# Normalising the first stage's input before the projections, fewer decay transfers, and bias tables on 128 partitions in a hybrid decoder step

## The chip, the cores and the metric

The kernel runs on one core of a Trainium2 chip. The metric is the device time of one execution in microseconds (us). PE is TensorE's matmul side, PEld its weight load, DVE is VectorE, ACT ScalarE, POOL GpSimd, and SP the engine whose queue issues most DMAs. Traces come from one execution under the hardware profiler.

## The reference

One inference step for a prompt of 512 positions and 8 samples of 4 new positions (544 columns together), width 1024, two layers. Layer A is a Mamba-2 SSD mixer, layer B an attention mixer over three dilated windows with one K/V computed after layer A. Cut to what matters here:

```python
def rmsnorm(x, g):
    y = x * lax.rsqrt(jnp.mean(x * x, axis=-1, keepdims=True) + NORM_EPS)
    return y * g

def ssd_mixer(h, conv_prev, ssm_init, g_norm, w_in, conv_w, conv_b, dt_bias, a_log, ...):
    u = rmsnorm(h, g_norm) @ w_in            # z, x|B|C and dt
    ...                                      # conv of width 4 over x|B|C, then silu
    dt = softplus(dt_raw + dt_bias)
    y, s_final = ssd_scan(xs * dt, dt * -exp(a_log), bm, cm, ssm_init)

def ssd_scan(xdt, adt, bm, cm, init):        # chunks of 128 positions
    a_cs = jnp.cumsum(A, axis=-1)
    seg = jnp.exp(jnp.where(tri, a_cs[..., :, None] - a_cs[..., None, :], -jnp.inf))
    chunk_decay = jnp.exp(a_cs[..., -1])
    ...

def group_bias(rel_bias, g):                 # a bias for each distance and head
    return rel_bias[:, g * KV_HEADS:(g + 1) * KV_HEADS][t5_bucket(dist)]
```

## The kernel before

Activations lie transposed, 1024 channels as 8 tiles of 128 partitions by 544 columns, and are worked on in two parts, columns 0 to 255 (HA) and 256 to 543. Each f32 product is made of three passes over split operands: a high part (xh, whi) rounded to the fast matmul type and the remainder (xl, wlo): high by high, high by low, low by high. A weight tile (`fetch_w`, L185; 512 KB into one of three `wraw` buffers) is split by ACT (whi, L196) and DVE or POOL (wlo, L197). One weight tile over all columns is 48 matmul steps.

**The first stage** (L299 to L457) makes the first three conv tiles, `first = [16, 20, 0]`. Its order is written out and held. It multiplies x by the gain only (`raw_high`, `raw_low`), and runs the passes on that; the squares are summed meanwhile, the inverse norm is spread over partitions with a matmul against a diagonal (`rstd_fin`, rp), and the products are multiplied by it when they leave PSUM (`evac`, cb). Then x is normalised in place (`x_mul`, L377) and split again (`x_high` L381, `x_low` L385) for `dt_proj` and all later tiles. POOL takes a part of the low splits (POOL_A, POOL_B) and the first weights' wlo. After `dt_proj` come four z passes and then conv and z tiles (`filler_a`).

**The decays** (`dt_chain`, L474 to L510) are computed on 128 partitions, 32 heads by four chunks. What every partition must see goes through DRAM: acd and ecd (prompt rows of t2 and t3), asd and esd (sample columns, 4 DMAs each), eld (last elements, 4 + 1 DMAs, one element at a time), and back as m, ea, as, es (per unit) and dec (once, broadcast). SP issues in order, and takes one of eight completion counters in turn for each DMA, so that an issue waits until the DMA eight places before it has landed. The SSD units (`ssm_chunk`, `ssm_quad`) start with transposes xp; `ms` (L728) is the first use of `as` on DVE.

**The bias tables** (`bias_tables`, L878 to L927) run in steps between the output and K/V projections: the table relt (96 columns, 32 a group, of which 8 are heads) times one-hot columns gives biases on 32 partitions. DVE copies them into ov (prompt, two halves) and bsr (samples), which share one buffer `tv`; rows 0 to 7 are written to bvd (each head 32 times) and bsd, and read back per head in layer B. xk (L858) is x for the residual.

An unwritten order is set by the framework's scheduler from the dependencies and its own estimates. The score loop of the samples (`sample`, L1193) runs over the key ranges outside and the four samples inside.

Of the kernel before, what the change touches and what calls it, by code (L numbers as in the profile page):

```python
# [12 lines left out]
F32 = mybir.dt.float32  # L13
# [5 lines left out]
D = 1024  # L19
SEQ = 512  # L20
# [102 lines left out]
def tile_yoco_step(  # L123
# [16 lines left out]
    def mm(*a, **k):  # L140
        pin(nc.tensor.matmul(*a, **k))  # L141
# [135 lines left out]
    acd = dram.tile([128, 128], F32, name="acd")  # L277
    ecd = dram.tile([128, 128], F32, name="ecd")
    asd = dram.tile([NH, 32], F32, name="asd")
    esd = dram.tile([NH, 32], F32, name="esd")  # L280
    eld = dram.tile([12, NH], F32, name="eld")
# [17 lines left out]
    dma(x_t[1][:, :, 0:HA], xT[:, 4:8, 0:HA])  # L299
    w_raw.append(fetch_w(w_in[1]))  # L300
    for i in range(2):
        dma(x_t[i][:, :, HA:T], xT[:, 4 * i:4 * i + 4, HA:T])
    w_raw.append(fetch_w(w_in[2]))
# [17 lines left out]
    def x_square(i, c0, c1):  # L321
        hold(nc.scalar.activation(sqx[i][:, :, c0:c1], x_t[i][:, :, c0:c1], AF.Square))

    def x_sum(i, c0, c1):
        sq = sqx[i][:, :, c0:c1]
        hold(nc.vector.tensor_tensor(sq[:, 0:2], sq[:, 0:2], sq[:, 2:4], op=ALU.add))
        hold(nc.vector.tensor_tensor(sq[:, 0], sq[:, 0], sq[:, 1], op=ALU.add))

    def x_means(ms, i, c0, c1, one=False):
        n = c1 - c0  # L330
        b0s = [min(128 * b, n - 128) for b in range((n + 127) // 128)]
        for b, b0 in enumerate(b0s):
            mm(ms[:, b:b + 1], sqx[i][:, 0, c0 + b0:c0 + b0 + 128], inv_d, start=i + b == 0, stop=one or i == 1,
               skip_group_check=True)
        return ms, n, b0s

    def evac(o, p, rs):
        if rs is None:
            nc.scalar.copy(o, p)  # L339
        else:  # L340
            hold(nc.vector.tensor_tensor(o, p, rs, op=ALU.mult))

# [3 lines left out]
    def conv_in(ti, pa, rs=None):  # L346
# [4 lines left out]
        evac(cb[:, 3:3 + HA], pa[:, 0:HA], None if rs is None else rs[:, 0:HA])  # L351
        return cb, cs

    def conv_in2(cbs, pb, rs=None):
        cb, cs = cbs
        evac(cb[:, 3 + HA:3 + SEQ], pb[:, 0:SEQ - HA], None if rs is None else rs[:, HA:SEQ])
        evac(cs[:, :, 3:7], by_row(pb, SEQ - HA), None if rs is None else by_row(rs, SEQ))
# [7 lines left out]
    def raw_high(k0, k1, c0, c1):  # L365
        for k in range(k0, k1):
            hold(nc.scalar.activation(part(x_h, k, c0, c1), part(x_t, k, c0, c1), AF.Copy, scale=g_a[:, k:k + 1]))

    def raw_low(k0, k1, c0, c1):
        for k in range(k0, k1):  # L370
            hold(nc.vector.scalar_tensor_tensor(part(x_l, k, c0, c1), part(x_t, k, c0, c1), g_a[:, k:k + 1],  # L371
                                                f32(part(x_h, k, c0, c1)), op0=ALU.mult, op1=ALU.subtract))

    def x_mul(k0, k1, c0, c1):
        for k in range(k0, k1):
            xk = part(x_t, k, c0, c1)
            hold(nc.vector.scalar_tensor_tensor(xk, xk, g_a[:, k:k + 1], rs_x[:, c0:c1], op0=ALU.mult, op1=ALU.mult))  # L377

    def x_high(c0, c1):
        for k in range(KD):  # L380
            hold(nc.scalar.activation(part(x_h, k, c0, c1), part(x_t, k, c0, c1), AF.Copy))  # L381

    def x_low(c0, c1, pool):
        for k in range(KD):
            hold((nc.gpsimd if k in pool else nc.vector).tensor_tensor(  # L385
                part(x_l, k, c0, c1), part(x_t, k, c0, c1), f32(part(x_h, k, c0, c1)), op=ALU.subtract))

    def passes(p, w, c0, c1, one=True, two=True, low_last=False):
        hi, lo = w
        o = p[:, 0:c1 - c0]  # L390
        second, third = ((lo, x_h), (hi, x_l)) if low_last else ((hi, x_l), (lo, x_h))
        for k in range(KD if one else 0):
            mm(o, hi[:, k, :], part(x_h, k, c0, c1), start=k == 0, stop=False)
            mm(o, second[0][:, k, :], part(second[1], k, c0, c1), start=False, stop=False)
        for k in range(KD if two else 0):
            mm(o, third[0][:, k, :], part(third[1], k, c0, c1), start=False, stop=k == KD - 1)

    def sums_of(c0, c1):
        ms = pss("ms")
        for i in range(2):  # L400
            sums = x_means(ms, i, c0, c1)
        return sums

    dga, dgb = tt("dgx"), tt("dgx")
    rs_x = const.tile([128, T], F32, name="rstd", tag="rstd", bufs=2)
    pinned[0] = True
    raw_high(0, 4, 0, HA)
    w_first = [split_w(w_raw[0], None, nc.gpsimd, True)]
    raw_high(4, 8, 0, HA)
    raw_low(0, 8, 0, HA)  # L410
    for i in range(2):
        x_square(i, 0, HA)
        x_sum(i, 0, HA)
    w_first.append(split_w(w_raw[1], None, nc.gpsimd, True))
    pp = [pj("pa"), pj("pb"), pj("pa")]
    passes(pp[0], w_first[0], 0, HA)
    x_square(0, HA, T)
    rpa = rstd_fin(*sums_of(0, HA), dga, later=True, keep=hold)
    raw_high(0, 4, HA, T)
    raw_low(0, 4, HA, T)  # L420
    w_first.append(split_w(w_raw[2], half("w2", F32R, (128, 2, 8, 128)), nc.gpsimd, True))
    passes(pp[1], w_first[1], 0, HA)
    hold(nc.scalar.copy(rs_x[:, 0:HA], rpa()[:, 0:HA]))
    x_square(1, HA, T)
    raw_high(4, 8, HA, T)
    passes(pp[2], w_first[2], 0, HA)
    cbs = [conv_in(first[i], pp[i], rs_x) for i in range(2)]
    x_sum(0, HA, T)
    raw_low(4, 8, HA, T)
    x_sum(1, HA, T)  # L430
    x_mul(0, 2, 0, HA)
    hold(nc.gpsimd.tensor_scalar(cvp, cvp, 0.5, None, op0=ALU.mult))
    hold(nc.gpsimd.tensor_scalar(g_gate, g_gate, 0.5, None, op0=ALU.mult))
    w_more = [split_w(fetch_w(w_in[3]), None, nc.gpsimd, True)]
    pb0 = pss("pb0")
    passes(pb0, w_first[0], HA, T, True, False)
    rpb = rstd_fin(*sums_of(HA, T), dgb, later=True, keep=hold)
    hold(nc.scalar.activation(warm, epst, AF.Tanh))
    passes(pb0, w_first[0], HA, T, False, True)
    hold(nc.scalar.copy(rs_x[:, HA:T], rpb()[:, 0:HB]))  # L440
    x_mul(2, 8, 0, HA)
    conv_in2(cbs[0], pb0, rs_x)
    cbs.append(conv_in(first[2], pp[2], rs_x))
    x_high(0, HA)
    x_mul(0, 8, HA, T)
    pb1 = pj("pb")
    passes(pb1, w_first[1], HA, T)
    conv_in2(cbs[1], pb1, rs_x)
    x_low(0, HA, POOL_A)
    w_more.append(split_w(fetch_w(w_in[4]), None, nc.gpsimd, True))  # L450
    pb2 = pj("pb")
    passes(pb2, w_first[2], HA, T)
    x_high(HA, T)
    x_low(HA, T, POOL_B)


    t0, t1, t2, t3, t4 = (tm[:, 136 * i:136 * i + 136] for i in range(1, 6))  # L457
    pads = tm[:, 816:1200].rearrange("p (a b) -> p a b", b=128)
    tok = ac.tile([128, 6, 3, NH], F32, name="tok")
# [14 lines left out]
    def dt_chain():  # L474
# [23 lines left out]
        dma(acd, t2[:, 0:128])  # L498
        dma(ecd, t3[:, 0:128])
        for j in range(4):  # L500
            rows = slice(32 * j, 32 * j + 32)
            dma(asd[:, 8 * j:8 * j + 8], t2[rows, 128:136])
            dma(esd[:, 8 * j:8 * j + 8], t3[rows, 128:136])
            dma(dap(eld, (4 + 2 * j) * NH, [[1, NH], [NH, 2]]), t3[rows, 131:136:4])
        dma(dap(eld, 0, [[1, 128], [1, 1]]), t3[:, 127:128])
        dma(dec, dap(eld, 0, [[0, 128], [1, 12 * NH]]))
# [4 lines left out]

    def tok_transposes():
        tp = pss("tp", (128, 4, 128))
# [99 lines left out]
    def ssm_chunk(g, c):  # L613
# [7 lines left out]
        dma(m_t, dap(acd, (32 * c + 8 * g) * 128, [[0, 128], [128, 8], [1, 128]]))  # L621
# [21 lines left out]
        if c:  # L643
            ea = wk.tile([128, 4, 128], F32, name="ea", bufs=1)
            for s in range(2):
                dma(ea[64 * s:64 * s + 64], dap(ecd, (32 * c + 8 * g + s) * 128, [[0, 64], [256, 4], [1, 128]]))
# [27 lines left out]
    def ssm_quad(g, q):  # L674
        xs, v, G = xs_t[g], v_t[g], grp[g]
        hs = slice(8 * g, 8 * g + 8)
        if q == 0:
# [118 lines left out]
    conv_in2(cbs[2], pb2, rs_x)  # L796
# [703 lines left out]
```

## Time and profile before

| | |
|---|---|
| median of 3 runs | 1017.63 us (1017.35 to 1018.21) |
| the profiled execution | 1013.88 us |
| its span, first to last instruction | 1012.0 us |
| mean granted TensorE clock | 0.972 |
| PE busy | 944.4 us, 93% of the span |
| DVE, ACT, POOL busy | 590.5, 446.1, 249.7 us |
| DMA moved | 159.93 MB, mean 158 GB/s |

Busy time is a sum over stages with different limits, so the table says only that PE is the engine to follow. What to read is where PE is idle, what ended each idle time, and at which clock it worked after it. An inferred releaser is the last event that a wait was waiting for. Rows of the timeline give start, duration, engine, line, operation, output and input, size and count, and in brackets the idle time before.

### The profile page before, as it was taken

What the parts mean: (1) busy time and instruction counts of PE and PEld (TensorE: products, weight loads), DVE (VectorE), ACT (ScalarE), POOL (GpSimd) and SP (SyncE); (2) the same over time, 40 slices, a digit from 0 to 9 for tenths busy, and PEclk for the clock granted to TensorE, in tenths of its full rate; (3) what the DMA queues carried; (4) which work ended last, traced back from release to release, by engine and by line L of the source; (5) the groups of instructions that cost most, each with busy time, mean ns of one, the idle gap of its engine ahead of it and who ended that gap; (6) DMA issues with size and microseconds to landing.
All of it is one profiled execution on the core that took longest, in us unless ns stands there. A gap on an engine that the chain in (4) does not pass through costs nothing.

```text
span 1012.0 us, 21657 instructions
## 1 busy us (share of the span) xinstructions
PE 944.4 (93%) x8811; PEld 872.6 (86%) x8811; DVE 590.5 (58%) x1216; ACT 446.1 (44%) x940; POOL 249.7 (25%) x344
## 2 busy tenths in 40 slices
PE   5895999899999998999756999999999999999996
PEld 5894888799888888999756999998888888888896
DVE  5983897998998797554432445334433434455532
ACT  6464745556555654322211223434344434445442
POOL 4641434834744633011000420000000000000451
PEclk9898999999999999999887999999999999999998
DMA  8126254354465532446454653666566567564412
GB/s 276 49 33 150 85 194 150 136 182 143 150 200 170 178 122 96 134 158 105 155 123 126 186 180 122 248 219 204 198 211 196 190 213 225 175 209 147 157 37 89
DMA packets 68171, 159.93 MB, mean 158 GB/s; under 512 B 19304, under 2 KB 33016, under 8 KB 67560
## 3 DMA queue, kind: packets, MB, share of 16 engines
q1 hardware_dynamic: 63096, 144.27, 45.7%
q10 hardware_dynamic: 2880, 9.44, 2.3%
q0 software_dynamic: 2096, 4.84, 1.8%
q8 instruction: 69, 1.13, 0.5%
q14 instruction: 30, 0.25, 0.1%
HBM read 134.83 MB, written 21.59 MB: 155 GB/s over the span
## 4 chain that ended last, share of the span: by engine, by line
PE 77%; DVE 9%; DMA 8%; ACT 2%; issue 2%; SPq 2%; POOL 0%; DVEq 0%; ACTq 0%
PE pa L141 28%; PE pb L141 27%; PE sp L141 3%; DMA bvd<-ov 3%; PE so L141 3%; PE pv L141 2%; PE s L141 2%; DMA xk<-xT 2%; DVE co L540 1%; PE yd L141 1%; DVE x L377 1%; PE csp L141 1%; DVE wlo L197 1%; PE w L144 1%; DMA as<-asd 1%
## 5 line engine op out<-in xcount | busy, mean ns | idle before, releaser
L197 DVE TENSOR_TENSOR wlo<-wraw,whi 128x1024 fp32r<-128x1024 f32 x99 | 123.8, 1251 | 89.7 <-ACT whi L196 89.4
L196 ACT ACTIVATE whi<-wraw 128x1024 fp32r<-128x1024 f32 x105 | 110.8, 1055 | 143.1 <-PE pb L141 90.4
L141 PE MATMUL pa<-xh,whi 128*128 128x256 f32 (+1 forms) x320 | 94.0, 296 | 10.3 <-ACT whi L196 8.3
L141 PE MATMUL pb<-xh,whi 128*128 128x288 f32 (+1 forms) x304 | 91.6, 303 | 3.9 <-ACT cb L339 3.9
L141 PE MATMUL pb<-xl,whi 128*128 128x288 f32 (+1 forms) x304 | 91.5, 303 | 0.0
L141 PE MATMUL pa<-xh,wlo 128*128 128x256 f32 (+1 forms) x320 | 90.7, 290 | 0.7 <-DVE wlo L197 0.7
L141 PE MATMUL pa<-xl,whi 128*128 128x256 f32 (+1 forms) x320 | 88.6, 291 | 0.5 <-DVE xl L371 0.5
L141 PE MATMUL pb<-xh,wlo 128*128 128x288 f32 (+1 forms) x304 | 87.3, 298 | 0.0
L141 PE MATMUL pb<-bh,wlo 128*128 128x288 f32 x256 | 77.7, 303 | 0.0
L141 PE MATMUL pb<-bl,whi 128*128 128x288 f32 x256 | 77.6, 303 | 0.0
L141 PE MATMUL pb<-bh,whi 128*128 128x288 f32 x256 | 77.0, 301 | 0.0
L1223 POOL COPY lse<-mxs 128x1 f32<-128x1 f32 x16 | 3.0, 186 | 291.0 <-DVE mxs L1221 291.0
L141 PEld LDWEIGHTS pa<-xh,whi 128*128 128x128 f32 x320 | 63.3, 198 | 12.4 <-ACT whi L196 8.3
L141 PE MATMUL pa<-bl,whi 128*128 128x256 f32 x256 | 74.0, 289 | 0.0
L141 PE MATMUL pa<-bh,wlo 128*128 128x256 f32 x256 | 73.9, 289 | 0.0
L141 PE MATMUL pa<-bh,whi 128*128 128x256 f32 x256 | 73.5, 287 | 0.0
L540 DVE SCALAR_TENSOR_TENSOR co<-cb,cvp,co 128x568 f32<-128x568 f32 x72 | 66.3, 921 | 0.9 <-ACT co L538 0.3
L141 PEld LDWEIGHTS pa<-xh,wlo 128*128 128x128 f32 x320 | 61.9, 195 | 2.0 <-DVE wlo L197 1.1
L141 PEld LDWEIGHTS pb<-xh,whi 128*128 128x128 f32 x304 | 58.9, 194 | 5.0 <-ACT cb L339 4.1
L141 PEld LDWEIGHTS pb<-xl,whi 128*128 128x128 f32 x304 | 58.8, 193 | 4.5 <-issue 4.4
L141 PEld LDWEIGHTS pa<-xl,whi 128*128 128x128 f32 x320 | 60.5, 195 | 2.2 <-issue 1.4
L141 PEld LDWEIGHTS pb<-xh,wlo 128*128 128x128 f32 x304 | 56.5, 190 | 2.2 <-issue 2.2
(360 smaller groups left out, 2785.3 us busy)
## 6 DMA issues: line engine op xcount, KB each, us to landing
wraw<-w_in SPq DMA_DIRECT2D x40, 512.0 KB
kc<-ck SPq DMA_DIRECT2D x32, 640.0 KB
vc<-cv SPq DMA_DIRECT2D x32, 640.0 KB
wraw<-wb SPq DMA_DIRECT2D x32, 512.0 KB
s<-s SPq DMA_DIRECT2D x16, 512.0 KB
m<-acd SPq DMA_DIRECT2D x16, 512.0 KB
ssmS<-s ACTq DMA_DIRECT2D x16, 512.0 KB
wraw<-w_out SPq DMA_DIRECT2D x16, 512.0 KB
```

Source lines behind the costliest of these rows:

```text
L141: pin(nc.tensor.matmul(*a, **k))
L144: pin(nc.tensor.transpose(*a))
L196: a = nc.scalar.activation(hi, raw, AF.Copy)
L197: b = lo_eng.tensor_tensor(lo, raw, f32(hi), op=ALU.subtract)
L377: hold(nc.vector.scalar_tensor_tensor(xk, xk, g_a[:, k:k + 1], rs_x[:, c0:c1], op0=ALU.mult, op1=ALU.mult))
L540: nc.vector.scalar_tensor_tensor(o, cb[:, k:k + n], cvp[:, ti, k:k + 1], o, op0=ALU.mult, op1=ALU.add)
L1223: nc.gpsimd.tensor_copy(lse[:, i16:i16 + 1], mx[:, 2:3])
```

## The change

It edits three places. In the first stage x's first part is loaded at the head of the queue, squares are summed over channels by matmuls against ones (msa, msb), the root and reciprocal are taken on all 128 partitions, and x is normalised and split before the first pass; ten matmuls on ones run at the start; POOL_A and POOL_B are gone, and ACT takes the products out of PSUM. The decays go out in aed and sed0, sed0 is copied to sed in another layout from DRAM to DRAM, and dec is made by a matmul. The bias table's columns are repeated 16 times, so that a bias lies on 128 partitions and bvd is written from all of them; `tv` has two buffers, and vt and hb share four. The description of the change also names the order of the decode scores; the diff has no line on that loop.

```diff
     x_t = [half("x0"), half("x1")]
+    for i in range(2):
+        dma(x_t[i][:, :, 0:HA], xT[:, 4 * i:4 * i + 4, 0:HA])
     gn = const.tile([128, 56], F32, name="gn")
     dma(gn, gains)
-    dma(x_t[0][:, :, 0:HA], xT[:, 0:4, 0:HA])
...
+    def x_sum(i, k, n, first_, last):
+        c0, c1 = ((0, HA), (HA, T))[i]
+        for kk in range(k, k + n):
+            mm(msx[i][:, 0:c1 - c0], ones, part(sqx, kk, c0, c1), start=first_ and kk == k, stop=last and kk == k + n - 1)
+
+    def x_rstd(i):
+        c0, c1 = ((0, HA), (HA, T))[i]
+        hold(nc.scalar.activation(rs_x[:, c0:c1], msx[i][:, 0:c1 - c0], AF.Sqrt, bias=epst, scale=1.0 / D))
+
+    def x_inv(c0, c1):
+        hold(nc.vector.reciprocal(rs_x[:, c0:c1], rs_x[:, c0:c1]))
...
+    wps = pss("wps")
+    for _ in range(10):
+        mm(wps[:, 0:128], ones, ones, start=True, stop=True)
     for i in range(2):
-        x_square(i, 0, HA)
-        x_sum(i, 0, HA)
+        sq, xa = sqx[i][:, :, 0:HA], x_t[i][:, :, 0:HA]
+        n = 4 - 2 * i
+        hold(nc.scalar.activation(sq[:, 0:n], xa[:, 0:n], AF.Square))
+        if i:
+            hold(nc.vector.tensor_tensor(sq[:, n:4], xa[:, n:4], xa[:, n:4], op=ALU.mult))
+        hold(nc.vector.tensor_tensor(sq[:, 0:2], sq[:, 0:2], sq[:, 2:4], op=ALU.add))
+        x_sum(0, 4 * i, 2, i == 0, i == 1)
+    x_rstd(0)
...
+    hold(nc.scalar.activation(hi, w_raw[0], AF.Copy))
+    x_inv(0, HA)
...
+    x_mul(0, 0, HA)
+    for k in range(KD):
+        if k + 1 < KD:
+            x_mul(k + 1, 0, HA)
+        x_high(k, 0, HA)
+        x_low(k, 0, HA)
+        square_b(k)
+        if k == 5:
+            w_first.append(split_w(w_raw[1], None, nc.gpsimd, True))
+    hold(nc.vector.tensor_tensor(lo, w_raw[0], f32(hi), op=ALU.subtract))
+    passes(pp[0], w_first[0], 0, HA, between=lambda k: x_sum(1, k, 1, k == 0, k == KD - 1))
+    x_rstd(1)
+    x_inv(HA, T)
     w_first.append(split_w(w_raw[2], half("w2", F32R, (128, 2, 8, 128)), nc.gpsimd, True))
...
+    for i in (1, 2):
+        passes(pp[i], w_first[i], 0, HA)
+    for i in range(3):
+        cbs.append(conv_in(first[i], pp[i]))
+        pb = pj("pb")
+        passes(pb, w_first[i], HA, T)
+        conv_in2(cbs[i], pb)
+    w_more = [split_w(fetch_w(w_in[i])) for i in (3, 4)]
...
-        dma(acd, t2[:, 0:128])
-        dma(ecd, t3[:, 0:128])
-        for j in range(4):
-            rows = slice(32 * j, 32 * j + 32)
-            dma(asd[:, 8 * j:8 * j + 8], t2[rows, 128:136])
-            dma(esd[:, 8 * j:8 * j + 8], t3[rows, 128:136])
-            dma(dap(eld, (4 + 2 * j) * NH, [[1, NH], [NH, 2]]), t3[rows, 131:136:4])
-        dma(dap(eld, 0, [[1, 128], [1, 1]]), t3[:, 127:128])
-        dma(dec, dap(eld, 0, [[0, 128], [1, 12 * NH]]))
+        t23 = tm[:, 136 * 3:136 * 5].rearrange("p (i c) -> p i c", i=2)
+        dma(aed[:].rearrange("i r c -> r i c"), t23[:, :, 0:128])
+        dma(sed0[:], t23[:, :, 128:136])
+        for i in range(2):
+            dma(dap(sed, i * NH * 32, [[32, NH], [8, 4], [1, 8]]), dap(sed0, 8 * i, [[16, NH], [16 * NH, 4], [1, 8]]))
+        for i, c in enumerate((127, 131, 135)):
+            nc.vector.tensor_scalar(dgs[:, i, :], ident, t3[:, c:c + 1], None, op0=ALU.mult)
...
+    def spread_decays():
+        dx = pss("dx")
+        mm(dx[:, 0:384], ones, dgs.rearrange("p a b -> p (a b)"), start=True, stop=True)
+        dv = dx[:, 0:384].rearrange("p (r j h) -> p r j h", r=3, j=4)
+        nc.scalar.copy(dec[:, 0:4], dv[:, 0])
+        nc.scalar.copy(dec[:, 4:12].rearrange("p (j r) h -> p r j h", r=2), dv[:, 1:3])
...
-                ov = wk.tile([32, VN // 2], F32, name="ov", tag="tv", bufs=1)
+                ov = wk.tile([128, VN // 2], F32, name="ov", tag="tv", bufs=2)
...
-                dma(bvd[:, :, q * (VN // 2):(q + 1) * (VN // 2)], ov[0:8, None, :].to_broadcast([8, 32, VN // 2]))
+                rows = bvd[:, :, q * (VN // 2):(q + 1) * (VN // 2)].rearrange("h (a r) v -> (h a) r v", r=2)
+                dma(rows, ov[:, None, :].to_broadcast([128, 2, VN // 2]))
                 continue
-            bsr = wk.tile([32, 2, SK], F32, name="bsr", tag="tv", bufs=1)
+            bsr = wk.tile([128, 2, SK], F32, name="bsr", tag="tv", bufs=2)
...
-            dma(bsd[:, g, t:t + 2, :], bsr[0:8])
+            dma(bsd[:, g, t:t + 2, :], bsr.rearrange("(h a) t k -> h a t k", a=16)[:, 0])
...
-        vt = wk.tile([128, T], F32, name="vt", bufs=3)
+        vt = wk.tile([128, T], F32, name="vt", tag="vt", bufs=4)
...
-        tmp = wk.tile([128, T], F32, name="hb", bufs=4)
+        tmp = wk.tile([128, T], F32, name="hb", tag="vt", bufs=4)
```

The scheduler's order moves in three places on which the prediction rests. First SP's queue at the end of the dt chain (tm holds its results; wraw is a weight tile, m and ea are the decays of the prompt's chunks, as and es those of the samples). Before, from the first decay write on, and from the last on:

```order
L498 DMA acd<-tm 128x128
L502 DMA asd<-tm 32x8
L499 DMA ecd<-tm 128x128
L503 DMA esd<-tm 32x8
L504 DMA eld<-tm 32x2x1
```

```order
L505 DMA eld<-tm 128x1
L187 DMA wraw<-w_in 128x1024 x2
L506 DMA dec<-eld 128x384
L621 DMA m<-acd 128x1024 x2
L187 DMA wraw<-w_in 128x1024
L646 DMA ea<-ecd 64x4x128 x2
L686 DMA as<-asd 128x256
```

Now:

```order
L476 DMA aed<-tm 128x2x128
L477 DMA sed_95<-tm 256x1x8
L188 DMA wraw<-w_in 128x1024
L479 DMA sed<-sed_95 128x1x8 x2
L605 DMA m<-aed 128x1024
L188 DMA wraw<-w_in 128x1024
L605 DMA m<-aed 128x1024
L630 DMA ea<-aed 64x4x128 x2
L670 DMA as<-sed 128x256
```

The element-wise writes and dec's load are gone; the copy from sed0 (`sed_95`) to sed stands ahead of m and of a weight tile, and `as` waits for it.

Second, DVE where the second half of bvd is finished (ov) and the samples' biases (bsr) begin, among the V tiles (vt). Before:

```order
L913 COPY ov<-bvp 32x160
L1045 SCALAR_TENSOR_TENSOR hb<-h_0_4699,gn,rstd 128x544
L967 TENSOR_TENSOR vt<-pb,rstd 128x288
L197 TENSOR_TENSOR wlo<-wraw,whi 128x1024
L966 TENSOR_TENSOR vt<-pa,rstd 128x256
L967 TENSOR_TENSOR vt<-pb,rstd 128x288
L197 TENSOR_TENSOR wlo<-wraw,whi 128x1024
L924 COPY bsr<-bs_5903 32x512
```

Now:

```order
L896 COPY ov<-bvp 128x160
L951 TENSOR_TENSOR vt<-pb,rstd 128x288
L908 COPY bsr<-bs_5863 128x512
L198 TENSOR_TENSOR wlo<-wraw,whi 128x1024
L950 TENSOR_TENSOR vt<-pa,rstd 128x256
L908 COPY bsr<-bs_5922 128x512
L951 TENSOR_TENSOR vt<-pb,rstd 128x288
L908 COPY bsr<-bs_5949 128x512
```

The first bsr copies stand right behind ov, one tile of V earlier, and hb has moved out.

Third, DVE's work ahead of the first stage's second part. Before, it splits x as it is, sums squares and builds the diagonal dgx:

```order
L371 SCALAR_TENSOR_TENSOR xl_107<-x_69,gn,xh_105 128x256 x4
L371 SCALAR_TENSOR_TENSOR xl_108<-x_70,gn,xh_106 128x256 x4
L326 TENSOR_TENSOR sqx_131<-sqx_131 128x2x256
L327 TENSOR_TENSOR sqx_131<-sqx_131 128x256
L326 TENSOR_TENSOR sqx_132<-sqx_132 128x2x256
L327 TENSOR_TENSOR sqx_132<-sqx_132 128x256
L262 RECIPROCAL sd<-sd 128x2
L265 TENSOR_SCALAR dgx<-ident,sd 128x128 x2
```

Now:

```order
L386 TENSOR_TENSOR sqx_129<-sqx_129 128x2x256
L385 TENSOR_TENSOR sqx_130<-x_70 128x2x256
L386 TENSOR_TENSOR sqx_130<-sqx_130 128x2x256
L353 RECIPROCAL rstd<-rstd 128x256
L357 SCALAR_TENSOR_TENSOR x_69<-x_69,gn,rstd 128x256 x2
L363 TENSOR_TENSOR xl_106<-x_69,xh_104 128x256
L357 SCALAR_TENSOR_TENSOR x_69<-x_69,gn,rstd 128x256
L363 TENSOR_TENSOR xl_106<-x_69,xh_104 128x256
```

The squares come first, and each tile of x is normalised one ahead of its low split.

More of the change, by code (lines that the diff above doesn't have):

```diff
@@ L276, in tile_yoco_step @@
     bsd = dram.tile([8, 3, TS, SK], F32, name="bsd")
[L277 to L281, printed above, removed]
+    aed = dram.tile([2, 128, 128], F32, name="aed")
+    sed0 = dram.tile([128, 2, 8], F32, name="sed0")
+    sed = dram.tile([2, NH, 32], F32, name="sed")
     vnd = dram.tile([NB, TS, ATH, 128], F32, name="vnd")
@@ L319, in tile_yoco_step, with conv_in @@
     sqx = [half("sqx0"), half("sqx1")]
[L321 to L341, printed above, removed]
     def by_row(t, c0):
         return t[:, c0:c0 + NB * TS].rearrange("p (b c) -> p b c", c=TS)
-    def conv_in(ti, pa, rs=None):
+    def conv_in(ti, pa):
         cb = tt("cb", 3 + SEQ + NB * 7)
@@ L374, in x_mul @@
[L374 to L386, printed above, removed]
@@ L388, in passes @@
-    def passes(p, w, c0, c1, one=True, two=True, low_last=False):
+    rs_x = const.tile([128, T], F32, name="rstd", tag="rstd", bufs=2)
+    msx = [pss("msa"), pss("msb")]
+    def x_sum(i, k, n, first_, last):
[5 more added lines that the diff above has]
+        hold(nc.scalar.activation(rs_x[:, c0:c1], msx[i][:, 0:c1 - c0], AF.Sqrt, bias=epst, scale=1.0 / D))
@@ L389, in passes @@
+    def passes(p, w, c0, c1, high=True, low=True, between=None):
         hi, lo = w
         o = p[:, 0:c1 - c0]
-        second, third = ((lo, x_h), (hi, x_l)) if low_last else ((hi, x_l), (lo, x_h))
-        for k in range(KD if one else 0):
+        for k in range(KD if high else 0):
             mm(o, hi[:, k, :], part(x_h, k, c0, c1), start=k == 0, stop=False)
-            mm(o, second[0][:, k, :], part(second[1], k, c0, c1), start=False, stop=False)
-        for k in range(KD if two else 0):
-            mm(o, third[0][:, k, :], part(third[1], k, c0, c1), start=False, stop=k == KD - 1)
@@ L398, in sums_of @@
[L398 to L405, printed above, removed]
+            mm(o, hi[:, k, :], part(x_l, k, c0, c1), start=False, stop=False)
+            if between:
+                between(k)
+        for k in range(KD if low else 0):
+            mm(o, lo[:, k, :], part(x_h, k, c0, c1), start=False, stop=k == KD - 1)
@@ new lines, in tile_yoco_step, with square_b @@
+    lo = wpool.tile([128, 8, 128], F32R, name="wlo", bufs=2)
+    w_first = [(hi, lo)]
+    hold(nc.scalar.activation(hi, w_raw[0], AF.Copy))
+    x_inv(0, HA)
+    pp = [pj("pa"), pj("pb"), pj("pa")]
+    def square_b(k):
+        hold(nc.scalar.activation(part(sqx, k, HA, T), part(x_t, k, HA, T), AF.Square))
+    x_mul(0, 0, HA)
[7 more added lines that the diff above has]
+            w_first.append(split_w(w_raw[1], None, nc.gpsimd, True))
@@ L449, in tile_yoco_step @@
[L449 to L454, printed above, removed]
+    x_mul(0, HA, T)
+    for k in range(KD):
+        if k + 1 < KD:
+            x_mul(k + 1, HA, T)
+        x_high(k, HA, T)
+        x_low(k, HA, T)
+    hold(nc.scalar.activation(warm, epst, AF.Tanh))
+    cbs = []
+    for i in (1, 2):
[5 more added lines that the diff above has]
+        conv_in2(cbs[i], pb)
```

92 lines of the change are left out of this document (29 added, 63 removed).

## The prediction

> **What bounds the kernel now.** I read the sums over the stages first. In a row of this view stand the stretch, its length, then busy time (and instructions) of PE, PEld, DVE, ACT and POOL, then the granted TensorE clock, the DMA share and GB/s. TensorE (PE) is nearly always busy; three stretches are not:
>
> ```profile
> 75.00:105.00 30.00, 17.84 (x123) 17.15 (x123) 12.87 (x23) 15.11 (x38) 3.08 (x10) 0.83 0.62 146
> 480.00:495.00 15.00, 9.93 (x61) 9.43 (x60) 4.81 (x7) 2.50 (x4) 1.35 (x1) 0.77 0.47 149
> 520.00:545.00 25.00, 6.45 (x42) 6.03 (x42) 4.06 (x6) 2.37 (x6) 0.18 (x1) 0.66 0.55 109
> ```
>
> PE stands for 30 - 17.84 = 12.2 us, 5.1 us and 18.6 us there. Behind each gap it also works at a lower clock:
>
> ```profile
> 95.00:100.00 5.00, 2.65 (x13) 2.65 (x14) 2.92 (x7) 4.11 (x9) 0.86 (x2) 0.50 0.09 26
> 100.00:105.00 5.00, 5.00 (x34) 5.00 (x34) 5.00 (x9) 4.75 (x14) 0.68 (x4) 0.81 0.34 105
> ...
> 485.00:490.00 5.00, 3.73 (x15) 3.44 (x16) 2.90 (x4) 1.47 (x3) 1.35 (x1) 0.50 0.51 188
> 490.00:495.00 5.00, 5.00 (x36) 5.00 (x36) 0.62 (x1) 0.15 (x1) 0.00 (x0) 0.89 0.01 3
> ...
> 540.00:545.00 5.00, 5.00 (x35) 4.99 (x35) 1.39 (x3) 0.90 (x3) 0.00 (x0) 0.77 0.50 172
> ```
>
> Busy time times (1 - clock) is lost again: 1.3 + 0.95 = 2.3 us behind the first gap, 1.9 + 0.55 = 2.4 behind the second, 1.2 (and 0.3 before it) behind the third. So the gaps cost **14.4, 7.5 and 20.1 us**. Next the waits, to see whom PE and those it waits for were waiting for (us in total, times, longest):
>
> ```profile
> PE bs L141 <- ACT bsr L925: 18.6, 1, 18.6
> ...
> ACT bsr L925 <- DMA bvd<-ov: 17.5, 1, 17.5
> ...
> PE pa L141 <- ACT whi L196: 12.3, 2, 8.3
> ...
> PE xp L144 <- DVE xs L543: 9.8, 1, 9.8
> ...
> ACT whi L196 <- DMA wraw<-w_out: 8.1, 1, 8.1
> ...
> ACT whi L196 <- DMA wraw<-w_in: 7.0, 1, 7.0
> ...
> DVE ms L728 <- DMA as<-asd: 6.7, 1, 6.7
> ```
>
> Every gap ends at a DMA. The chain of waits (start, length) gives their places (its first two rows are for the first stage below):
>
> ```profile
> 2.21 6.35 DMA x<-xT
> ...
> 21.53 0.43 PE rp L141 x2
> ...
> 70.81 8.80 DMA eld<-tm
> ...
> 84.47 9.35 DMA as<-asd
> ...
> 465.33 19.38 DMA xk<-xT
> ...
> 512.11 26.81 DMA bvd<-ov
> ```
>
> The first gap is the decays' way through DRAM: the weights wraw were queued behind the element-wise eld writes, and then DVE stood at `ms` until `as` landed at 93.8. The other two are the two writes of the bias table bvd: the second is waited for directly (one `tv` buffer), and xk and weights sit behind the first.
>
> **The change part by part.**
>
> *Bias tables.* bvd is 256 x 4672 B = 1.20 MB in each half, written from 8 partitions in 26.8 us (45 GB/s); now the same bytes leave from 128. The nearest row is h1d, 1.11 MB from 128 partitions, issued at 445.1; beside it a stretch within the first bvd write:
>
> ```profile
> 445.00:450.00 5.00, 5.00 (x42) 5.00 (x42) 1.40 (x2) 0.65 (x2) 1.37 (x1) 1.00 0.87 269
> ...
> 470.00:475.00 5.00, 5.00 (x42) 5.00 (x41) 1.10 (x2) 0.27 (x2) 1.36 (x1) 1.00 0.57 77
> ```
>
> At 269 GB/s the write takes 4.4 us; the bounds are this and the old 26.8. I take 4.4, since h1d goes from SBUF to DRAM on the same queue with the same bytes. With two `tv` buffers the first bsr waits for the first bvd write alone, over 50 us old; bsr of the next pair waits for the second write and comes one weight tile (6.0 us) after it, so 4.4 us are covered. The matmuls stream as many columns as before for 128 instead of 32 outputs, and DVE copies as many columns per partition: nothing. vt and hb sharing four buffers moves hb's first multiplications behind the last vt, where DVE is half idle: nothing. Term: 7.5 + 20.1 = **-27.6 us**, bounds 0 and -27.6.
>
> [...]
>
> *Decays.* 16 DMAs become 4, and `dec` comes from a matmul of the diagonal tiles dgs (three DVE operations, two copies). But `as` now lies behind two hops: sed0 is written, and sed copied from it, DRAM to DRAM in 32-byte pieces. What a small piece costs:
>
> ```profile
> 60.27 0.33 SPq L498 DMA_DIRECT2D acd<-tm  x1
> ...
> 64.87 2.00 SPq L504 DMA_DIRECT2D eld<-tm  x1
> ```
>
> The second waits for ecd, eight issues before it, so acd, asd and ecd, 288 pieces or 18 on each of 16 engines, took 6.6 us: 0.37 us a piece. The last eld with the three small writes just before it (16 pieces an engine, 69.9 to 79.6) gives 0.6. Bounds 0.3 and 0.6; I take 0.4, the row with pieces of 32 and 512 B. Then aed and sed0 (16 pieces an engine each) take 12.8 us, the sed copies 6.4 us, and m, ea and one weight tile, queued ahead of `as`, about 6. The start and the need come from the first stage.
>
> *First stage.* x is normalised first; the products no longer are multiplied by the inverse norm, and x is not rebuilt afterwards. Rows:
>
> ```profile
> 5.60 1.70 ACT L367 ACTIVATE xh<-x,gn 128x256 fp32r<-128x256 f32 x4 [3.37 <-DMA x<-xT]
> 10.20 1.99 ACT L322 ACTIVATE sqx<-x 128x1024 f32<-128x1024 f32 x2
> ...
> 27.12 0.87 DVE L377 SCALAR_TENSOR_TENSOR x<-x,gn,rstd 128x256 f32<-128x256 f32 x2
> 28.49 0.18 DVE L262 RECIPROCAL sd<-sd 128x3 f32<-128x3 f32 x1 [0.50 <-ACT sd L261]
> ...
> 43.57 3.26 DVE L385 TENSOR_TENSOR xl<-x,xh 128x256 fp32r<-128x256 f32 x9
> 52.99 1.00 DVE L482 RECIPROCAL tm<-tm 128x136 f32<-128x136 f32 x1
> ```
>
> x's first part lands at 5.60 now, its second, behind a weight tile, at 8.56: 1.48 us for each 512 KB. Put first (0.45 us earlier) and without the tile between, they land at 5.15 and 6.63; squares, sums and the two last sum matmuls (rp: 0.43 us, 0.8 at half clock) end at 9.6, the root at 10.0. A reciprocal grows by 0.82 / 133 = 6.2 ns a column: 1.75 us for 256 columns, 1.95 for 288. Eight times (0.43 + 0.36) for x and xl follow, to 18.1, and one weight split of ACT in between, to 19. POOL's split of the second weights then meets DVE:
>
> ```profile
> 13.21 2.84 POOL L197 TENSOR_TENSOR wlo<-wraw,whi 128x1024 fp32r<-128x1024 f32 x1 [2.50 <-ACT whi L196]
> ...
> 13.88 2.45 DVE L327 TENSOR_TENSOR sqx<-sqx 128x256 f32<-128x256 f32 x1
> ...
> 29.25 6.53 DVE L377 SCALAR_TENSOR_TENSOR x<-x,gn,rstd 128x256 f32<-128x256 f32 x6
> ```
>
> Beside POOL these run at 2.45 and 1.09 us in place of 0.4. So wlo of the first weights ends at 21.2, the second reciprocal at 23.2, and the second half's eight pairs (0.45 + 0.36, with 1.2 for POOL) at 30.9. From there PE waits for nobody:
>
> ```profile
> 41.98 2.36 PE L141 MATMUL dp<-x,wd 128*32 128x8 f32 x62 [0.23 <-DVE x L377]
> 44.27 0.58 PE L141 MATMUL pa<-xh,whi 128*128 128x256 f32 x1
> ...
> 57.79 0.28 PE L141 MATMUL pa<-xh,whi 128*128 128x256 f32 x1
> ...
> 580.24 3.19 PE pb L141 x24
> 583.44 2.83 PE pa L141 x24
> ```
>
> 1.3 for the rest of the first pass, two of 3.19, dt_proj with 128 instructions at 38 ns (4.9), four z passes (12.0): 55.5 us, where now it is 57.79. Term: **-2.3 us**. If PE is cold through half of this, or POOL blocks longer, it is +1; if x and the squares overlap better, -5.
>
> *Back to the decays.* The dt chain starts at 43.5 and needs 10 to 12 us (mixed with conv work, 12 now): aed is issued at about 54.4, so `as` lands at 54.4 + 0.4 + 12.8 + 0.9 + 6.4 + 6 = 80.9. PE meets the first SSD transposes xp 200 steps (25.1 us) and the small transposes (1.6 us) after 55.5, at 82.2; DVE must be at `ms` 3.4 us before (now 93.9 against xp at 97.35), at 78.8. So 2 of the 14.4 us stay: **-12.4 us**; with 0.3 us a piece nothing stays, with 0.6 it is 12 us.
>
> The sum: -27.6 - 12.4 - 2.3 = -42.3 us on the profiled execution's 1013.9, hence 971.6. The runs' median lies 3.7 us above that execution, so I predict **975 us**.
>
> **The rivals.**
>
> *A: the decays still stall PE.* Small writes go at 0.6 us a piece: 16 + 16 pieces add 9.6 us, and PE stands for about 11.6. For it speaks the eld row (8.8 us for 128 pieces), against it that PE has 25 us of other work. Then 975 + 10 = 985 us. [...] No row here has a DRAM-to-DRAM copy.
>
> *B: the first stage becomes longer.* Normalising first puts squares, root, reciprocal and POOL's splits in one line before the first product. If DVE stands through both splits and PE stays at half clock until 31 us, +3 in place of -2.3: 980 us. For it: PE has only short bursts until then. Against it: two splits are 4.8 us in all, half of it in the sum.
>
> *C: bvd stays slow,* because DRAM and not the source's partitions set its rate. Then xk and the weights wait as before, and bsr of the second pair waits 26.8 - 6.0 = 21 us: 975 + 27.6 = 1002 us. Against it: h1d's rate.
>
> *D, slower than before: the sed copies hold up SP's queue.* SP issues in order, so the weights behind the wait for sed0 and `as` behind sed come late, and all the rest with them. To eat up 42 us, the copies must land after 78.8 + 42 us, that is take some 48 instead of 6.4 us (3 us a piece); from there the kernel is slower, at double that by about 50 us, 1065. No row shows a piece above 1.1 us.
>
> *E: nothing.* The description speaks of the order of the decode scores, but no line of the diff touches the score loop, which runs as before: 0 us of any term.
>
> **How the numbers follow.** Forecast (966 to 980) 0.62, A 0.14, B 0.12, C 0.06, D 0.04, and 0.02 for A, B and C together, which comes out near 1017. The range, 964 to 988, takes in the best ends (-27.6 - 14.4 - 5 gives 970 by the median; some stalls elsewhere may shrink too) and A and B, and leaves out C and D. Measurements tell 0.2%, 2 us, from no change. Faster: 0.94; same 0.02; slower 0.04.
>
> **What would show it.** PE's idle time in 480 to 545 gone and no wait on bvd; bvd landing within 6 us of its issue; z's last pass ending near 55.5 us; `ms` waiting on `as` for under 3 us; PE's busy time up by under 6 us. If `as` lands after 85, it is A; if xk lands 19 us after its issue again, C.

## The result and the profile after

The changed kernel takes **970.95 us** (median of 4 runs, 969.6 to 973.13), the kernel before on the same chip 1017.92 us: ratio 0.9538, 95% interval 0.9518 to 0.9559, faster by 47.0 us. Forecast were 975 us, 964 to 988. A second set of 5 runs gave 969.48 us against 1017.15 us, ratio 0.9516 (0.9491 to 0.9540).

The sums over the same stretches as before, in the kernel after (stretch, length, busy time and count of PE, PEld, DVE, ACT, POOL, granted clock, DMA share, GB/s):

```profile
75.00:105.00 30.00, 30.00 (x242) 27.74 (x241) 24.55 (x40) 24.90 (x63) 11.34 (x26) 1.00 0.28 93
...
480.00:495.00 15.00, 15.00 (x118) 14.40 (x117) 7.80 (x16) 5.42 (x10) 1.03 (x2) 1.00 0.69 228
...
520.00:545.00 25.00, 25.00 (x201) 24.78 (x201) 13.31 (x20) 7.30 (x14) 14.66 (x30) 1.00 0.67 196
```

All three gaps are closed, at full clock. PE is busy for 944.0 us as before (944.4), now 97% of a span of 971.4 us. The longest waits of PE that are left, in the table of waits:

```profile
PE pb L141 <- ACT cb L326: 3.9, 1, 3.9
...
PE pa L141 <- ACT xh L360: 3.3, 1, 3.3
...
PE yos L141 <- DMA s<-s: 2.9, 1, 2.9
```

The first lies at 166.6 us (a gap of the same length stood at 183.5 us before), the second at 10.2 us in the first stage. The third is new in size: it ends at 248.75 us, and where yos waited for s before, PE stood for 0.3 us (in changed_again, the second set, for 1.6). None is on bvd, bsr or `as`. SP's timeline shows the new decay transfers and one bvd write:

```profile
54.84 0.38 SPq L476 DMA_DIRECT2D aed<-tm  x1
55.27 0.63 SPq L477 DMA_DIRECT2D sed<-tm  x1
56.24 0.33 SPq L188 DMA_DIRECT2D wraw<-w_in  x1
57.22 1.24 SPq L479 DMA_DIRECT2D sed<-sed  x2
...
61.97 0.56 SPq L670 DMA_DIRECT2D as<-sed  x1
...
490.89 0.55 SPq L900 DMA_DIRECT2D bvd<-ov  x1
...
498.50 0.65 SPq L911 DMA_DIRECT2D bsd<-bsr  x1
```

The copy from sed0 waits for sed0's landing, and SP issues it 1.95 us behind sed0: the hop that the forecast put at 12.8 us with aed. By the trace's records of single packets those of `as` ended at 71.3 us, and DVE takes it without waiting, behind work of its own:

```profile
77.77 1.66 DVE L524 SCALAR_TENSOR_TENSOR co<-cb,cvp,co 128x568 f32<-128x568 f32 x2
79.34 0.29 DVE L712 TENSOR_TENSOR ms<-as,tok 128x128 f32<-128x128 f32 x1
```

### The profile page after: what moved, and what is told of

It is laid out like the page before. It is cut to its first block, busy times and chain, and to the rows that moved or that the text cites. A ratio compares the mean times of both kernels' runs of the same rounds, so it can differ in the third digit from the quotient of the medians.

```text
span 971.4 us, 21631 instructions
## 1 busy us (share of the span) xinstructions
PE 944.0 (97%) x8833; PEld 871.5 (90%) x8833; DVE 581.1 (60%) x1194; ACT 443.2 (46%) x939; POOL 234.8 (24%) x334
## 4 chain that ended last, share of the span: by engine, by line
PE 85%; DVE 7%; ACT 3%; DMA 3%; POOL 1%; issue 1%; DVEq 0%; SPq 0%; ACTq 0%
PE pa L141 32%; PE pb L141 31%; PE sp L141 3%; PE so L141 3%; PE pv L141 2%; PE s L141 2%; PE yd L141 1%; DVE co L524 1%; PE csp L141 1%; PE w L144 1%; PE yo L141 1%; PE ptp L144 1%; PE yos L141 1%; PE xp L144 1%; DVE wlo L198 1%
## 5 line engine op out<-in xcount | busy, mean ns | idle before, releaser
L198 DVE TENSOR_TENSOR wlo<-wraw,whi 128x1024 fp32r<-128x1024 f32 x101 | 126.1, 1248 | 81.6 <-ACT whi L197 78.1
L141 PE MATMUL pa<-xl,whi 128*128 128x256 f32 (+1 forms) x320 | 90.7, 286 | 1.2 <-DVE xl L363 1.2
L141 PE MATMUL pa<-xh,wlo 128*128 128x256 f32 (+1 forms) x320 | 85.0, 283 | 0.0
L141 PEld LDWEIGHTS pa<-xh,whi 128*128 128x128 f32 x320 | 60.8, 190 | 6.3 <-ACT xh L360 3.8
L141 PEld LDWEIGHTS pa<-xh,wlo 128*128 128x128 f32 x320 | 58.0, 188 | 1.3 <-issue 0.9
```

The costliest lines, as they stand in the source:

```text
L198: b = lo_eng.tensor_tensor(lo, raw, f32(hi), op=ALU.subtract)
```

## The experiments

Each kernel was timed beside the kernel before on its chip.

| run | median us | before | ratio (95% interval) |
|---|---|---|---|
| before_bias | 987.94 | 1017.68 | 0.9707 (0.9667 to 0.9746) |
| before_decays | 1004.24 | 1017.68 | 0.9863 (0.9823 to 0.9903) |
| before_first | 1007.46 | 1017.68 | 0.9899 (0.9866 to 0.9933) |
| after_old_first | 975.24 | 1017.68 | 0.9585 (0.9549 to 0.9621) |
| dec_by_matmul | 1004.36 | 1017.88 | 0.9844 (0.9793 to 0.9894) |
| eld_kept | 1011.90 | 1017.88 | 0.9943 (0.9920 to 0.9965) |
| eld_apart | 1003.36 | 1017.88 | 0.9849 (0.9809 to 0.9888) |
| one_buffer | 971.27 | 1016.44 | 0.9548 (0.9521 to 0.9575) |
| eight_rows | 995.11 | 1016.44 | 0.9784 (0.9758 to 0.9811) |
| eight_rows_spread | 972.66 | 1016.44 | 0.9573 (0.9546 to 0.9599) |
| changed_again | 969.48 | 1017.15 | 0.9516 (0.9491 to 0.9540) |
| splits_on_dve | 970.81 | 1017.15 | 0.9532 (0.9507 to 0.9556) |

### The three parts alone

The diff was cut into its three parts, each put alone on the kernel before; and the changed kernel got the old first stage back. No code beyond the diff.

> The kernel before with the bias tables' edit alone. If the terms of the sum add up as they stand on record, the two bvd gaps (7.5 and 20.1 us) go and the first gap stays: about 1017.9 - 27.6 = 990 us, each bvd write landing within 6 us of its issue. Rival: the writes get fast, but half of the gain is given back later, since the weights behind bvd meet another limit: 1000 us or more.

> The kernel before with the decays' edit alone. By the price on record (0.4 us for each small piece on an engine) aed goes out at 60.3 us, as lands at 86.8, needed at about 81: a stall of 5.7 us stays, 1017.9 - 8.7 = 1009 us. By the trace of the changed kernel, where sed0 and sed landed within 2 us each, nothing stays: 1017.9 - 14.4 = 1003.5 us.

> The kernel before with the new first stage alone. By the end of the z passes in the traces (57.4 against 57.8 us) it is worth 0.4 us by itself; but it sends the decays out 5.4 us earlier (54.8 against 60.3), so the first gap, still there, shrinks by as much: about 1012.5 us. Rival: the gap is set by something other than the decays' start, and stays: 1017.5 us.

> The changed kernel with the first stage of the kernel before (the other two edits stay). If the first stage is worth the 0.4 us of the z passes' end, 971.4 us, the same as the changed kernel; if it carries the 4.7 us by which the measured gain (47.0) exceeds the sum on record (42.3), about 975.6 us; if it costs time, under 970 us.

The bias tables bring 29.7 us (25.8 to 33.9 by the interval), as forecast, and the decays 13.4 us (9.9 to 18.0), near the 14.4 that the changed kernel's trace had promised; the 8.7 us by the price on record lie just outside. The stage sums of before_decays are plainer, with PE busy through the whole stretch of the first gap:

```profile
75.00:105.00 30.00, 30.00 (x244) 27.98 (x242) 24.14 (x39) 23.48 (x57) 9.35 (x22) 1.00 0.31 99
```

The first stage alone brings 10.2 us (6.8 to 13.6), more than expected. A row of its DVE timeline and its stage sums show how:

```profile
84.01 0.29 DVE L706 TENSOR_TENSOR ms<-as,tok 128x128 f32<-128x128 f32 x1 [2.15 <-DMA as<-asd]
```
```profile
75.00:105.00 30.00, 25.00 (x184) 23.84 (x184) 21.89 (x36) 21.10 (x50) 7.16 (x19) 0.89 0.44 145
```

The first write of the decays goes out at 53.05 instead of 60.27 us, so `ms` gets `as` at 84.0 instead of 93.9, and PE stands for 5.0 us instead of 12.2. The first stage and the decays thus close the same gap, and their gains can't be added. The times agree with that but don't prove it: alone the three sum to 53.4 us, and together they bring 47, but the three intervals together reach from 42.5 to 65.5. With that gap gone the old first stage costs 4.3 us, 975.24 against the changed kernel's 970.95; the two intervals (0.9549 to 0.9621 and 0.9518 to 0.9559) just overlap, so it is anything from nothing to 10 us; the changed kernel's second set (0.9491 to 0.9540) lies apart from it, which speaks for a cost.

### What the small writes cost

Three versions of the decays, all on the kernel before. In dec_by_matmul:

```diff
-            dma(dap(eld, (4 + 2 * j) * NH, [[1, NH], [NH, 2]]), t3[rows, 131:136:4])
-        dma(dap(eld, 0, [[1, 128], [1, 1]]), t3[:, 127:128])
-        dma(dec, dap(eld, 0, [[0, 128], [1, 12 * NH]]))
+        for i, c in enumerate((127, 131, 135)):
+            nc.vector.tensor_scalar(dgs[:, i, :], ident, t3[:, c:c + 1], None, op0=ALU.mult)
```

and spread_decays as in the change. eld_kept leaves the two writes in and drops the load of dec alone. eld_apart also moves every element to a place of its own, 512 bytes from the next:

```diff
-    eld = dram.tile([12, NH], F32, name="eld")
+    eld = dram.tile([12, NH, 128], F32, name="eld")
-            dma(dap(eld, (4 + 2 * j) * NH, [[1, NH], [NH, 2]]), t3[rows, 131:136:4])
+            dma(dap(eld, (4 + 2 * j) * NH * 128, [[128, NH], [NH * 128, 2]]), t3[rows, 131:136:4])
-        dma(dap(eld, 0, [[1, 128], [1, 1]]), t3[:, 127:128])
+        dma(dap(eld, 0, [[128, 128], [1, 1]]), t3[:, 127:128])
```

> The kernel before, with dec made by the matmul and the five eld writes and dec's load taken out; acd, ecd and the eight writes of asd and esd stay. If the eld writes of 4-byte elements make the first gap, it goes whole: 1017.7 - 14.4 = 1003.3 us, and wraw behind them lands within 4 us. If every small piece costs, as the price on record has it (0.37 us a piece for asd and esd too, 16 pieces an engine), 6 us of them stay in the way and the gap shrinks to about half: 1010 us.

> As dec_by_matmul, but the five eld writes are still made as before, one 4-byte element after the other into 1.5 KB of DRAM, and nobody reads them: work that the kernel does not need. If the writes disturb the weight loads behind them, weights land about 9 us late as before and 1012 us or more results; if the wait for eld to land (dec's load) was the cost, there is no gap: 1003.3 us.

> As eld_kept, but each 4-byte element goes to a place 512 bytes from the next (196 KB of DRAM), read by nobody. If it is the number of small pieces that costs, the time is that of eld_kept; if it is that all of them fall into the same few hundred bytes, it is that of dec_by_matmul, 1003.3 us.

Without eld the gap is gone, 13.5 us, although asd and esd still go out in eight writes of 32-byte pieces: so it was not the number of small pieces. With eld's writes kept and read by nobody, 7.5 us of it come back. With the same 384 elements 512 bytes apart, none of it does. The stage sums, first of eld_kept, then of eld_apart:

```profile
70.00:75.00 5.00, 5.00 (x43) 5.00 (x42) 3.90 (x6) 3.21 (x6) 1.81 (x5) 1.00 0.48 17
75.00:80.00 5.00, 5.00 (x39) 4.68 (x38) 2.66 (x5) 0.68 (x1) 0.54 (x2) 1.00 0.67 34
...
85.00:90.00 5.00, 2.02 (x13) 1.46 (x12) 2.85 (x3) 4.46 (x15) 1.90 (x4) 1.00 1.06 324
90.00:95.00 5.00, 1.06 (x5) 1.07 (x6) 2.37 (x7) 2.52 (x6) 0.22 (x1) 0.58 0.59 145
```
```profile
70.00:75.00 5.00, 5.00 (x42) 5.00 (x42) 3.90 (x6) 3.14 (x6) 1.71 (x5) 1.00 0.84 294
75.00:80.00 5.00, 5.00 (x39) 4.68 (x38) 3.89 (x6) 2.93 (x7) 1.48 (x3) 1.00 1.06 310
```

The last two columns tell it. The loads are issued at 72.6 us in eld_kept and at 69.6 in eld_apart, so the second row of each is the fair one: the DMA engines are at work for two thirds of the time and move 34 GB/s, where the same loads behind spread writes run at 310. It is the weight loads behind eld that crawl. The records of single DMA packets give the first weight tile behind eld's writes (128 packets of 4 KB, counted from the moment named):

```
before         from 71.93 us: last ends 82.95, longest packet 5.9 us
eld_kept       from 72.50 us: last ends 83.10, longest packet 5.0 us
eld_apart      from 69.50 us: last ends 72.94, longest packet 1.2 us
dec_by_matmul  from 64.30 us: last ends 67.36, longest packet 0.7 us
```

And eld itself lands late. The chain of waits of eld_kept:

```profile
72.08 7.96 DMA eld<-tm
80.04 0.02 issue
80.06 11.22 DMA as<-asd
```

Although nobody reads eld there, SP still waits for its landing, since each issue waits for the one eight places before: the issue of `as`, eight behind the last eld, comes at 80.06 us, when that eld has landed (80.04). From SP's table of waits in eld_kept (L656 issues ea, L696 `as`):

```profile
SPq L656 <- DMA eld<-tm: 1.9, 1, 1.9
SPq L696 <- DMA eld<-tm: 1.6, 1, 1.6
```

So the first gap had two causes: adjacent 4-byte writes, which land late and stall what is read behind them (7.5 us, eld_kept against dec_by_matmul, these waits of SP included), and the load of dec, at which SP waited for their landing with m, ea and `as` behind it (6.0 us, the kernel before against eld_kept). Why adjacent writes do this the runs don't show.

### Which part of the bias edit matters

Three versions of the changed kernel. one_buffer has `bufs=1` for the three `tv` tiles. eight_rows has the tables and the write of the kernel before, with `bufs=2`. eight_rows_spread writes from 8 partitions that lie apart:

```diff
-                rows = bvd[:, :, q * (VN // 2):(q + 1) * (VN // 2)].rearrange("h (a r) v -> (h a) r v", r=2)
-                dma(rows, ov[:, None, :].to_broadcast([128, 2, VN // 2]))
+                vs = slice(q * (VN // 2), (q + 1) * (VN // 2))
+                if q == 0:
+                    dma(bvd[:, :, vs], ov.rearrange("(h a) v -> h a v", a=16)[:, 0, None, :].to_broadcast([8, 32, VN // 2]))
+                else:
+                    for i in range(2):
+                        dma(bvd[4 * i:4 * i + 4, :, vs], ov[64 * i:64 * i + 61:20, None, :].to_broadcast([4, 32, VN // 2]))
```

> The changed kernel with one tv buffer in place of two; bvd is still written from 128 partitions. The second write was issued at 490.9 and landed at 497.1 us, and in the trace before PE worked on for 8.7 us after that issue: so one buffer would do and the rate alone carries the term: 971 us. Rival: the second buffer is needed to cover the landing, each write is then waited for: 4 to 9 us more, 975 to 980 us.

> The changed kernel with the bias tables on 32 partitions and bvd written from partitions 0 to 7 as before, but with two tv buffers. If the source's partitions set the rate, each packet takes 0.7 us again and a write some 24 us: xk and the weights wait (7.5 us), and the second pair of bsr waits for the second write, about 15 us: 971 + 22 = 993 us. Rival: the buffer was the point; with two of them PE no longer waits: under 980 us.

> The changed kernel with bvd still written from 8 partitions, but spread: the first half from partitions 0, 16, 32 to 112, the second from 0, 20, 40, 60, 64, 84, 104, 124 (in two DMAs). If the number of source partitions sets the rate, packets take 0.7 us in both and the time is that of eight_rows, about 993 us. If not their number but where they lie counts, the first write is about twice as fast as from partitions 0 to 7 (0.35 us a packet, 12 us) and the second as fast as from 128 (0.18 us, 5 us): no gap, 971 us. [...]

One buffer does as well as two (971.27 against 970.95 us). Two buffers with the old write lose 23.8 us against one_buffer, beside the two writes; the chain of waits of eight_rows:

```profile
449.13 19.57 DMA xk<-xT
...
496.40 28.78 DMA oh<-ohs x2
```

xk waits behind the first write as before, and beside the second it is now the one-hot loads (oh) of the following step that come late. That second wait is not the one expected: the copies to bsr waited for a bvd write for 1.2 us only, not for 15. The 4672-byte packets of the writes, from the trace's records (256 for each write):

```
                   write 1: median, first to last   write 2
before             708 ns, 23.20 us                 708 ns, 23.86 us
eight_rows         705 ns, 23.10 us                 708 ns, 24.05 us
eight_rows_spread  354 ns, 11.27 us                 180 ns, 14.55 us (two DMAs)
one_buffer         180 ns,  5.77 us                 180 ns,  4.93 us
the changed one    180 ns,  5.45 us                 180 ns,  4.93 us
```

Eight partitions each time, and three speeds: it is where the partitions lie that counts. From 0 to 7 a packet takes 708 ns, from 0, 16, 32 to 112 half of it (354), from 0, 20, 40, 60 (and 64 to 124) a quarter (180), as from 128. The 1.20 MB of the first write went out at 52 GB/s from 0 to 7 (23.20 us), at 106 from the spread set (11.27 us) and at 219 from 128 (5.45 us). That the two sets would be twice and four times as fast no earlier run had shown; these packets do. Why the position counts no run shows. One half of the expectation fell: the second write, in two DMAs issued 2.2 us apart (485.61 and 487.76 us), took 14.55 us, not 5. By the table's medians and lengths 3.2 of its packets ran at a time (256 x 0.18 / 14.55), against 8.0 in the first write; why no more did, the runs don't show. That cost nothing that can be measured (972.66 against 971.27 us).

### The first stage

splits_on_dve takes the low splits of the second and third weights from POOL and gives them to DVE:

```diff
-        if k == 5:
-            w_first.append(split_w(w_raw[1], None, nc.gpsimd, True))
     hold(nc.vector.tensor_tensor(lo, w_raw[0], f32(hi), op=ALU.subtract))
+    w_first.append(split_w(w_raw[1], None, nc.vector, True))
...
+        if k == 2:
+            hold(nc.vector.tensor_tensor(w2[:, 1], w_raw[2], f32(w2[:, 0]), op=ALU.subtract))
```

> The changed kernel as it is, once more, as the measure for the next run: its profiled execution had PE at a clock of 0.78 to 0.88 between 30 and 40 us, and dt_proj's end at 45.1 us, where three other kernels with the same first stage have 42.5 to 43.8. If that was one slow execution, dt_proj ends near 43 us here; the median is 971 us either way, and with the old first stage it was 975.2.

> The changed kernel with the low splits of the second and third weights (wlo of w_first 1 and 2) made by DVE instead of POOL, after the first weights' wlo and after the third pair of the second half. If POOL's splits hold up DVE (two xl took 2.72 us and two x 2.16 us beside them, 2.3 and 1.2 us more than alone), and ACT's whi before them 0.6 us, the last xl ends about 3 us earlier, at 30.3 us, and the kernel takes 1 to 3 us less than the changed one: 968 to 970 us. Rival: DVE's own 2.4 us for the two splits and PE's earlier work eat it: 971 us.

DVE's timeline, first of changed_again, then of splits_on_dve:

```profile
18.54 2.73 DVE L363 TENSOR_TENSOR xl<-x,xh 128x256 fp32r<-128x256 f32 x2 [0.61 <-ACT xh L360]
...
25.13 2.16 DVE L357 SCALAR_TENSOR_TENSOR x<-x,gn,rstd 128x288 f32<-128x288 f32 x2
...
32.15 1.05 DVE L363 TENSOR_TENSOR xl<-x,xh 128x288 fp32r<-128x288 f32 x2
...
43.58 0.36 DVE L452 TENSOR_SCALAR tm<-dp,dcs 128x136 f32<-128x136 f32 x1 [3.57 <-PE dp L141]
```
```profile
16.88 0.99 DVE L363 TENSOR_TENSOR xl<-x,xh 128x256 fp32r<-128x256 f32 x2
...
22.65 0.95 DVE L357 SCALAR_TENSOR_TENSOR x<-x,gn,rstd 128x288 f32<-128x288 f32 x2
...
29.90 1.05 DVE L363 TENSOR_TENSOR xl<-x,xh 128x288 fp32r<-128x288 f32 x2
...
41.35 0.36 DVE L455 TENSOR_SCALAR tm<-dp,dcs 128x136 f32<-128x136 f32 x1 [3.58 <-PE dp L141]
```

The pairs that took 2.73 and 2.16 us beside POOL take 0.99 and 0.95. In changed_again it is one operation of each pair that stands until POOL's is over: POOL's splits run from 18.28 to 20.65 and from 24.14 to 26.52 us, the first xl of that pair from 18.54 to 20.93, the first x from 25.13 to 26.84.

The dt chain starts 2.2 us earlier, but not all of that is the edit's. The sums of squares ahead of it ran faster in this execution; PE's rows, again first of changed_again:

```profile
6.41 3.75 PE L141 MATMUL msa<-sqx,ones 128*128 128x256 f32 x8 [0.72 <-DVE sqx L386]
```
```profile
6.55 1.13 PE L141 MATMUL msa<-sqx,ones 128*128 128x256 f32 x4 [0.97 <-DVE sqx L386]
8.02 1.13 PE L141 MATMUL msa<-sqx,ones 128*128 128x256 f32 x4 [0.34 <-DVE sqx L386]
```

So DVE's first reciprocal starts at 9.69 instead of 10.70 us, before the edit does anything. one_buffer has the first stage of changed_again, had the same short sums, and its reciprocal starts at 9.70. Its dt chain:

```profile
42.60 0.36 DVE L452 TENSOR_SCALAR tm<-dp,dcs 128x136 f32<-128x136 f32 x1 [3.57 <-PE dp L141]
```

Against it the edit brings 1.25 us: the stall beside POOL is gone, and DVE's own two splits take part of it back. The timed runs show no gain: 970.81 against 969.48 us, with intervals that overlap, which is where the rival had put it (971). No faster version can be claimed.

## Why the prediction was right, and where not

**Bias tables: right, in mechanism and size.** On record -27.6, measured alone -29.7 (-33.9 to -25.8). The writes' packets took 5.45 and 4.93 us where 4.4 stood, and were covered. Counted from the issue they ended after 7.9 and 6.2 us, so the sign "within 6 us of its issue" was missed, at no cost: nobody waited. Nor did the wider table cost time: for 504 columns a matmul took 0.39 us with 32 outputs and with 128, and DVE's copy to ov 0.67 and 0.68 us. eight_rows, with the second buffer and the old speed, is 23.8 us slower than one_buffer: most of the term is the speed. The second buffer was not needed. Rival C is out.

**Decays: right in direction, one price wrong.** The forecast let 2 of 14.4 us stay, since it priced a small piece at 0.4 us on an engine, so that `as` landed at 80.9. Its last packet ended at 71.3. The step that failed is the price. The 0.37 us came from a stall of SP, from 64.87 to 66.87, that was read as a wait for ecd; by the trace's records of semaphore events acd, the first asd and ecd had all landed by 62.8 us (what SP stood for there isn't shown). What was late was the first eld, issued at 62.07: it landed at 68.65, in eld_apart the same write took 1.5 us (63.35 to 64.82). The 0.6 us came from a wait in which eld's writes stood too, and both were put down to asd's and esd's pieces. The 512 pieces of 32 bytes of sed0 and sed, on average 32 for each of the 16 engines, ran from 56.5 to 60.6 us with the wait between the hops: an estimated 0.13 us each at most (4.1 / 32). What was dear were adjacent 4-byte elements (1011.90 us in eld_kept, 1003.36 in eld_apart). The same evidence takes away rival A: sed's pieces of 32 bytes were quick, and so were eld_apart's pieces of 4 bytes. Rival D needed 48 us for the copies; sed's two copies and all before them were done 5.4 us after sed0's issue.

**First stage: right in size, by two errors that cancel.** On record were 30.9 us for the last xl, 43.5 for the start of the dt chain, 55.5 for the end of the z passes, 2.3 us less than before. In changed_again the last xl ends at 33.2 us, 2.3 us late: the first root came 0.7 us later than reckoned, one xl stood 2.0 us behind POOL's split where the sum left about 1, and DVE waited 0.75 us for the second root. But PE has less left to do behind it (10.4 us to the start of the dt chain, 12.6 on record), and the dt chain starts at 43.58 and the last tanh of the z passes at 55.9 us (57.5 in the changed kernel's first profiled execution). The end of z's last multiplication (the fourth uz) can be compared over the runs: 59.2 to 61.2 us in seven traces with the old first stage, mean 60.2; 56.9 to 59.6 us in six with the new, mean 58.0. That is -2.2 us. The profiled execution of the changed kernel, with 59.55, is the latest of the six, and its clock shows why:

```profile
30.00:35.00 5.00, 4.13 (x19) 2.97 (x18) 3.14 (x8) 4.17 (x8) 0.00 (x0) 0.88 0.00 0
35.00:40.00 5.00, 5.00 (x32) 5.00 (x31) 3.24 (x4) 3.09 (x7) 1.06 (x3) 0.78 0.29 105
```

Busy time times (1 - clock) is 4.13 x 0.12 + 5 x 0.22 = 1.6 us. changed_again has 1.00 in both stretches, and here the dt chain starts 1.6 us later, at 45.19. Rival B (the stage becomes longer) had its mechanism, POOL and DVE in each other's way, and not its result.

**The sum.** -42.3 was forecast, from the profiled execution; from profiled execution to profiled execution it is -40.8 (1013.88 to 973.13) and with changed_again's (969.67) -44.2; the medians say -47.0 and -47.7. The 2 us too many left to the decays are part of the difference. The rest would fit the base, though that was only argued: the profiled execution before lay 3.7 us under its median, and the forecast carried that distance over to the changed kernel, whose profiled executions lie at its median or above. Why the executions of the kernel before differ was not tried.

**E** stands as written: no line touches the score loop, and from the first to the last of layer B's score matmuls (sp and s) it takes 302.5 us before and 303.3 after.

## What to carry to other kernels

Count a transfer's source partitions by where they lie, not by how many they are (here a packet took 708 ns from partitions 0 to 7, 354 and 180 from two sets of eight that lie apart): a write from few rows was made fast here by spreading those rows, and by making the matmul in front of it produce them on all partitions; neither cost anything measurable (972.66 us spread, 971.27 and 970.95 us from 128). Single 4-byte elements written side by side to DRAM were paid for here by whoever read next on the same queue (34 GB/s behind them, 310 behind elements 512 bytes apart); build such values on the chip (1004.36 us against 1011.90), or write them apart (512 bytes did, 1003.36 us). Where two edits close the same gap, measure each with the other in place before adding their gains.

## What was not expected

- 384 adjacent 4-byte writes slowed the weight loads behind them to 34 GB/s (eld_kept, 75 to 80 us) and kept the first 512 KB tile for some ten microseconds, with single 4 KB packets of up to 5.9 us; 512 bytes apart they cost nothing measurable (1003.36 against 1004.36 us without them).
- A copy from DRAM to DRAM in 32-byte pieces was cheap: sed0 and both copies together took from 55.3 us to 60.6 us, issue to last packet, with a weight tile of 512 KB issued between them.
- The same first stage ended its dt_proj between 42.5 and 45.1 us in six executions. The 45.1 is the one with the granted clock at 0.78 to 0.88 between 30 and 40 us; the other five had 1.00 there and ended by 43.8, the two earliest (42.5 and 42.6) with the short sums of squares.
